# A decoder step on one Trainium2 core: fifteen input tiles made in the mixers' idle buffers, with in-place FFN input, weight sums on GpSimd and another order of the down-projection

## The chip, the cores and the metric

The kernel runs on one core of a Trainium2 chip. The core has a matrix engine (TensorE, PE in the profile; its weight loads are PEld), three elementwise engines (VectorE = DVE, ScalarE = ACT, GpSimd = POOL) and SyncE (SP), which here does nothing but issue transfers (DMA). The engines run side by side and meet through semaphores. On-chip memory is SBUF for operands and eight PSUM banks for matrix products. The metric is the device time of one execution, in microseconds.

## What is computed

One layer of a hybrid decoder, for 2048 prompt tokens and 8 x 8 sample tokens, model width 1024, all in float32:

```python
h = rmsnorm(x, norm_mix_w) * (1 + sc1) + sh1
proj = h @ w_in
qkv, z, b_raw, a_raw, sq, sk, sv = split(proj)
o_dn  = deltanet_mixer(qkv, z, b_raw, a_raw, ...)
o_swa = window_attention(sq, sk, sv, ...)
x = x + g1 * (concat(o_dn, o_swa) @ w_out)
h = rmsnorm(x, norm_ffn_w) * (1 + sc2) + sh2
u = causal_dwconv(h @ ffn_w_up) + ffn_conv_b
gate, up = split(u)
x = x + g2 * ((silu(gate) * up) @ ffn_w_down)
y = rmsnorm(x, final_norm_w)
```

`sh`, `sc` and `g` come from a small product of the conditioning vector (adaLN). The layer also returns the mixers' and the convolutions' states.

## The kernel before

**Products.** Every float32 operand is split into a rounded part and a rest ("hi" and "lo", `th`/`tl`, `wh`/`wl`), and every product is three matrix products. The split costs a copy on ACT and a subtraction on DVE or POOL for each tile. Tokens lie in the free dimension, features in the 128 partitions, so x is eight tiles (k = 0 to 7) by tokens.

**Order.** The tokens are worked in two halves (`HALVES`): the first has blocks of 512 and 512 tokens, the second of 384, 384 and 320, the last block holding the 64 sample tokens. The stages are: an opening stage (adaLN, statistics, first columns of the input projection), the rest of the first half's input projection (columns 12 to 21) beside the first steps of its mixers, the second half's input projection beside the first half's mixers, output projection and FFN up-projection of the first half, the same for the second half, then the down-projection for all tokens. `beside(steps, filler, share)` weaves elementwise-heavy mixer steps with products. Each step is a Python generator; `lockstep` advances several in turn, `chain` one after the other, `spaced` slows one down. The order in which a program line is reached is an input to a tile scheduler, which fixes each engine's instruction order before the run. Each engine, and SP's issue of transfers, then goes through its own list in order. A buffer (a tile with a tag in a pool, `bufs` of them in turn) is given out again when its last user is done; memory of a closed pool likewise.

**Places that the change touches.**

- `affine_h` (line 239) makes the projection's input h from x for one block: for each k it loads a tile of x into a "cv" buffer (line 263; there are five, `CV = 5`, in pool `gw`), scales it on DVE (line 264), adds the bias on ACT (line 266) and makes hi and lo. For odd k the subtraction is on POOL, after a separate ACT copy; for even k, ACT adds the bias while it makes hi, and DVE finishes lo. The sample tokens come as one tile `hst` (line 249), also a "cv" buffer, on which DVE does a multiplication (line 251), the bias addition and the subtraction. For the FFN, `src` can be a list of tiles that already lie in SBUF; the result still goes to a "cv" buffer.
- `second` (called when columns 12 to 21 of the first half are nearly done) calls `affine_h` for the second half: block 0 and a part of block 1 first, the rest when the first half's h is free.
- `in_evac` (from line 600) and `conv_block` (lines 530 to 548) empty a PSUM bank of the input projection and of the FFN: a copy (line 537), a scaled copy into a "cv" buffer (line 542 for the FFN) and, on DVE, the taps of the convolution (line 547). Lines 603 and 608 are the evacuation of the columns of z, sk and sv. Line 806 is a small DVE result in the mixers that a product of line 785 needs.
- The mixers' pool `mp` is opened before the first half's first mixer steps. Its tiles xz, qs, kh, kl, u, o, nl, pt and PT belong to attention and to the state scan, which start only after those steps (line 933 loads qs, 939 kl, 657 kq).
- `weight_sums` (line 1621) makes the sums of the down weights that the Winograd form of the down-projection needs: for each of 11 units two loads of 128 x 1024 into one buffer `suv`, four DVE additions of 128 x 512 (lines 1632 to 1635), two stores to `ws_d` (line 1638). Six units run in the opening stage (pool `sa`), five beside the sample tokens' mixers. On POOL in the opening stage run the square sums of `x_rstd` for the second half.
- `up_quarters` runs the second half's FFN up-projection and stores its results, token sums and E (line 1496) to HBM.
- `down_phase` (line 1648) goes through the tokens in two passes (`ip` 0 and 1), each with the seven products of the table `DOWN`. A row names the weight operand, the token operand, the token group of its form (the second is 64 tokens narrower in the second pass), whether it opens new banks, and the output blocks to which its result is added. Each product has 11 units i; a unit loads, splits and multiplies a weight tile (`wr`) and a token tile (`tr`). `T2 = B22 - T1` and `T4 = T1 + E` are formed on the way from two loads each (`tr` and `tx`, lines 1707 and 1712). Pool `ds` holds `wr`, `tr` and the splits, pool `dr` holds `tx`, the output blocks `x` (two buffers each) and the statistics. `out` adds a product to x (`residual`, line 1263 within it), and from the fourth row on a block is complete and its squares are summed. `norm` is the final norm and the store of y; it runs beside later products. Products 3 and 4 of the second pass use four banks, the others eight.

Of the kernel before, what the change touches and what calls it, by code (L numbers as in the profile page):

```python
# [22 lines left out]
P = 128  # L23
D = 1024
KT = 8
# [69 lines left out]
def kernel(  # L95
# [133 lines left out]
    def h_tile(hf, bi):  # L229
# [3 lines left out]
        return [t[:, a:a + KT * n].rearrange("p (k n) -> p k n", k=KT) for t in h_at]  # L233

    def affine_h(hb, bi, hf, branch, rB, src, ks=range(KT), pool_too=lambda k: k % 2, smp=None):

# [20 lines left out]
        for k in ks:  # L257
            h, l = hi[:, k, :np_], lo[:, k, :np_]
            t = x = gw.tile([P, 512], F32, tag="cv", name="ht", bufs=CV)[:, :np_]
            if isinstance(src, list):  # L260
                x = src[k][:, :np_]
            else:
                nc.sync.dma_start(x, src[k, :, c0:c0 + np_])
            nc.vector.scalar_tensor_tensor(t, x, S[:, k, 0:1], rB[:, :np_], ALU.mult, ALU.mult)
            if pool_too(k):
                nc.scalar.activation(t, t, AF.Identity, bias=B[:, k, 0:1], scale=1.0)
                nc.scalar.copy(h, t)
                nc.gpsimd.tensor_tensor(l, t, h.bitcast(F32), ALU.subtract)
            else:
                nc.scalar.activation(h, t, AF.Identity, bias=B[:, k, 0:1], scale=1.0)  # L270
                nc.vector.scalar_tensor_tensor(l, t, B[:, k, 0:1], h.bitcast(F32), ALU.add, ALU.subtract)  # L271
            yield True
# [1347 lines left out]

    def weight_sums(units, pool):

        tt = nc.vector.tensor_tensor
        cut = lambda t: (t[:, :D // 2], t[:, D // 2:])
        for i in units:
# [16 lines left out]

    DOWN = [("A11", "B11", 1, True, [(0, 1)]), ("S2", "T2", 1, False, [(0, 2)]), ("S3", "T3", 2, False, [(1, 1), (1, 2)]),
            ("S1", "T1", 2, True, [(1, 2)]), ("S4", "B22", 2, False, [(0, 2)]), ("A22", "T4", 1, True, [(1, 1)]),
            ("A12", "B21", 1, True, [(0, 1)])]
    NM = KT // 2

    def down_phase(ds, dr, pd):
# [28 lines left out]
        def load(tag, src, n, most, bufs):  # L1677

            raw = (dr if tag == "tx" else ds).tile([P, most], F32, tag=tag, name=tag, bufs=bufs)[:, :n]
            fetched[:] = [nc.sync.dma_start(raw, src).ins]  # L1680
            return raw
# [7 lines left out]

        w, t = {}, {}  # L1690

# [6 lines left out]
        def get_t(q, i, r):  # L1698

            if (q, i, r.start) in t:  # L1700
                return
            name = DOWN[q % ND][1]
            get = lambda tag, name, r, bufs: load(tag, t_src(q, name, i, r), r.stop - r.start, big, bufs)
            if name == "T2":
                raw, more = get("tr", "T1", r, RAWS), get("tx", "B22", slice(r.start, min(r.stop, PW)), RAWS)
                c = more.shape[1]
                nc.vector.tensor_tensor(raw[:, :c], more, raw[:, :c], ALU.subtract)
                if c < raw.shape[1]:
                    nc.scalar.mul(raw[:, c:], raw[:, c:], -1.0)
            elif name == "T4":  # L1710
                raw, more = get("tr", "T1", r, RAWS), get("tx", "E", r, RAWS)
                nc.vector.tensor_tensor(raw, raw, more, ALU.add)
            else:
                raw = get("tr", name, r, RAWS)
            t[q, i, r.start] = halves(ds, "t", raw, big, DR)

        def blocks_of(q, g=None):

            if q < ND or q % ND in (3, 4):
                return [slice(0, PW)]  # L1720
# [51 lines left out]
        for q in range(Q):  # L1772
# [26 lines left out]
            def out(m, s):  # L1799
                for og, tg in outs:  # L1800
# [3 lines left out]
                    residual(v, acc[m, s], n, n - LS if q >= ND and r.stop > PW else n, G[:, NM * og + m], v, dr)  # L1804
                    if j < 3:
                        continue
# [13 lines left out]
            def load_x():  # L1820
# [3 lines left out]
                o = need.pop(0)  # L1824
                x[o] = dr.tile([P, NM, big], F32, tag=f"x{o[0]}{o[1]}", name=f"x{o[0]}{o[1]}", bufs=2)
                with tc.issue_after(fetched[0]):
# [32 lines left out]
            elif j == 5:  # L1859
                finish = norm(*late, free[-2:], wait=2 - ip)  # L1860
            elif j == 6:
                late = (1, 0, PW, x, sums[1], cols[1])
            elif j == 2 and ip:
                finish = norm(*late, free[-2:], wait=2)
        rest(finish)
# [21 lines left out]
    with ExitStack() as main:  # L1887
# [12 lines left out]
        with ExitStack() as es:  # L1900
# [71 lines left out]
            for bi in range(2):  # L1972
                for m in range(2):
# [5 lines left out]
            chain(*[spaced(ada_cols([(c, k + q) for q in range(4)], ac, st, at_bank), 2) for c in range(2, 6) for k in (0, 4)],  # L1979
                  spaced(weight_sums(range(6), sa), 2)),  # L1980
            chain(bias_tables(sa), gates(0, h, ic["wb"], ip), *[x_rstd(1, bi, rBs[bi], sa, st_bank) for bi in range(3)]))
# [42 lines left out]
        with ExitStack() as es:  # L2024
            mp = new_pool(es, "mp", bufs=2, side="right")
            filler = inproj(0, h, ic, range(12, 22), freed=second, turn=(0, 2))
            inverse_tiles(mp)
            beside(ahead(0, mp), filler, SHARE[0])
            rest(filler)
# [21 lines left out]
        with ExitStack() as es:  # L2051
            sp = new_pool(es, "sp", side="right")
            beside(lockstep(sample_delta(sp), sample_attend(sp), weight_sums(range(6, KH), sp)), filler, SHARE[2])
        with ExitStack() as es:
# [121 lines left out]
```

## Time and profile before

| | us |
|---|---|
| runs shown, in order | 2650.94, 2656.68, 2646.79 |
| median of these | 2650.94 |
| the profiled execution | 2652.56 |
| its span in the trace | 2650.8 |
| mean granted PE clock in it | 0.99 |

The trace is of one execution on the one core, so its span, and not the median, goes with every duration read from it. In a timeline row the first number is the start in us from the begin of the span, the second the duration, and a bracket at the end gives the idle time of the engine before it and what ended that. In a row of groups (line, engine, operation, result <- operands, shape, count) the numbers after the first bar are busy us and mean ns of one, after the second bar the idle time ahead of them. SPq rows are issues of transfers by SP, DMA rows the transfers themselves. The granted clock is the share of full speed that TensorE's throttle allowed in a stretch.

### The profile page before, as it was taken

What the parts mean: (1) busy time and instruction counts of PE and PEld (TensorE: products, weight loads), DVE (VectorE), ACT (ScalarE), POOL (GpSimd) and SP (SyncE); (2) the same over time, 40 slices, a digit from 0 to 9 for tenths busy, and PEclk for the clock granted to TensorE, in tenths of its full rate; (3) what the DMA queues carried; (4) which work ended last, traced back from release to release, by engine and by line L of the source; (5) the groups of instructions that cost most, each with busy time, mean ns of one, the idle gap of its engine ahead of it and who ended that gap; (6) DMA issues with size and microseconds to landing.
All of it is one profiled execution on the core that took longest, in us unless ns stands there. A gap on an engine that the chain in (4) does not pass through costs nothing.

```text
span 2650.8 us, 45631 instructions
## 1 busy us (share of the span) xinstructions
PE 2564.9 (97%) x16424; PEld 2223.7 (84%) x16424; DVE 1838.0 (69%) x3657; ACT 1284.4 (48%) x3124; POOL 757.6 (29%) x677
## 2 busy tenths in 40 slices
PE   7999989999999899999999999999999999999998
PEld 5677878888897787777777789999999997889988
DVE  7475469887443677888868664886777666676676
ACT  5453355564342455455444353554555554554343
POOL 2031133233332412223211123335555520020012
PEclk9999989999999999999999999999999999999999
DMA  7787454334456253343226357424555459678673
GB/s 288 247 301 236 134 151 118 101 97 115 106 176 205 103 144 98 105 108 102 76 92 215 130 181 225 144 67 156 171 170 186 166 183 302 214 237 279 214 250 130
DMA packets 325327, 445.31 MB, mean 168 GB/s; under 512 B 83267, under 2 KB 207268, under 8 KB 324836
## 3 DMA queue, kind: packets, MB, share of 16 engines
q1 hardware_dynamic: 325100, 442.39, 52.7%
q8 instruction: 129, 2.11, 0.3%
q14 instruction: 98, 0.80, 0.1%
HBM read 322.74 MB, written 120.57 MB: 167 GB/s over the span
## 4 chain that ended last, share of the span: by engine, by line
PE 70%; DVE 12%; DMA 9%; ACT 3%; issue 3%; SPq 2%; POOL 1%; DVEq 0%; POOLq 0%; ACTq 0%
PE up_ps L339 15%; PE dn_ps L1795 15%; PE in_ps L339 12%; PE uq_b L1585 5%; PE op_ps L339 4%; PE uq_c L1585 2%; PE uq_u L1585 2%; PE uq_g L1585 2%; DVE ev L547 2%; PE pv_ps L1007 1%; PE uq_a L1585 1%; DMA mt<-mixd 1%; PE as_ps L970 1%; DVE w_lo L331 1%; DMA suv<-in_w_downT_dram 1%
## 5 line engine op out<-in xcount | busy, mean ns | idle before, releaser
L339 PE MATMUL in_ps<-hi,w_hi 128*128 128x512 f32 (+2 forms) x880 | 320.4, 367 | 10.0 <-ACT ev L608 5.6
L339 PE MATMUL up_ps<-hi,w_hi 128*128 128x512 f32 (+2 forms) x808 | 315.0, 390 | 7.3 <-ACT cv L542 7.3
L339 PE MATMUL in_ps<-lo,w_hi 128*128 128x512 f32 (+2 forms) x880 | 316.6, 360 | 2.4 <-DVE lo L271 2.0
L339 PE MATMUL in_ps<-hi,w_lo 128*128 128x512 f32 (+2 forms) x880 | 314.9, 358 | 0.0
L339 PE MATMUL up_ps<-lo,w_hi 128*128 128x512 f32 (+2 forms) x808 | 313.9, 388 | 0.0
L339 PE MATMUL up_ps<-hi,w_lo 128*128 128x512 f32 (+2 forms) x808 | 311.8, 387 | 0.0
L1795 PE MATMUL dn_ps<-th,wh 128*128 128x512 f32 (+2 forms) x796 | 272.2, 343 | 4.5 <-DVE x L1263 4.2
L1795 PE MATMUL dn_ps<-tl,wh 128*128 128x512 f32 (+2 forms) x796 | 272.2, 342 | 3.6 <-DVE tl L1687 3.6
L1795 PE MATMUL dn_ps<-th,wl 128*128 128x512 f32 (+2 forms) x796 | 270.8, 342 | 0.0
L331 DVE TENSOR_TENSOR w_lo<-w_raw,w_hi 128x1024 fp32r<-128x1024 f32 x115 | 145.7, 1267 | 82.8 <-ACT w_hi L330 81.3
L330 ACT CAST w_hi<-w_raw 128x1024 fp32r<-128x1024 f32 x126 | 132.0, 1047 | 145.9 <-PE op_ps L339 52.2
L339 PEld LDWEIGHTS in_ps<-hi,w_hi 128*128 128x128 f32 x880 | 166.6, 190 | 36.7 <-issue 7.8
L339 PEld LDWEIGHTS in_ps<-lo,w_hi 128*128 128x128 f32 x880 | 167.1, 190 | 26.2 <-issue 7.6
L339 PEld LDWEIGHTS up_ps<-hi,w_hi 128*128 128x128 f32 x808 | 152.6, 189 | 41.9 <-issue 8.6
L339 PEld LDWEIGHTS up_ps<-lo,w_hi 128*128 128x128 f32 x808 | 152.7, 189 | 35.1 <-issue 10.7
L339 PEld LDWEIGHTS in_ps<-hi,w_lo 128*128 128x128 f32 x880 | 166.8, 190 | 15.6 <-issue 1.6
L339 PEld LDWEIGHTS up_ps<-hi,w_lo 128*128 128x128 f32 x808 | 152.4, 189 | 31.4 <-issue 5.3
L1795 PEld LDWEIGHTS dn_ps<-th,wh 128*128 128x128 f32 x796 | 150.7, 190 | 21.9 <-DVE x L1263 3.9
L1795 PEld LDWEIGHTS dn_ps<-tl,wh 128*128 128x128 f32 x796 | 150.9, 190 | 19.1 <-DVE tl L1687 3.9
L1795 PEld LDWEIGHTS dn_ps<-th,wl 128*128 128x128 f32 x796 | 150.8, 189 | 15.6
L1686 ACT CAST wh<-wr 128x512 fp32r<-128x512 f32 x149 | 92.1, 618 | 143.7 <-PE dn_ps L1795 115.5
L547 DVE SCALAR_TENSOR_TENSOR ev<-rb,cw,ev 128x512 f32<-128x512 f32 (+2 forms) x180 | 132.3, 739 | 31.4 <-ACT ev L540 29.6
(547 smaller groups left out, 6493.5 us busy)
## 6 DMA issues: line engine op xcount, KB each, us to landing
w_raw<-in_w_upT_dram SPq DMA_DIRECT2D x50, 512.0 KB
wada<-in_w_ada_dram SPq DMA_DIRECT2D x48, 512.0 KB
w_raw<-in_w_inT_dram SPq DMA_DIRECT2D x44, 512.0 KB
wr<-ws_d SPq DMA_DIRECT2D x88, 256.0 KB
w_raw<-in_w_outT_dram SPq DMA_DIRECT2D x34, 512.0 KB
d<-act_d SPq DMA_DIRECT2D x33, 512.0 KB
wr<-in_w_downT_dram SPq DMA_DIRECT2D x66, 256.0 KB
tr<-T_d SPq DMA_DIRECT2D x66, 256.0 KB
```

Of the source, the lines that this page charges most:

```text
L330: nc.scalar.copy(hi, raw)
L331: (eng or nc.vector).tensor_tensor(lo, raw, hi.bitcast(F32), ALU.subtract)
L339: nc.tensor.matmul(ps[:, :n], a[:, k, :], b[:, k, :n], start=first is not False and k == ks[0] and i == 0, stop=last is not False and k == ...
L547: nc.vector.scalar_tensor_tensor(out, src(j), w[:, j:j + 1], out, ALU.mult, ALU.add)
L970: nc.tensor.matmul(banks[v][:, 256 * g:256 * g + 256 - P * k0], qs[:, 2 * (g0 + g) + v], t[:, v, :2 - k0].rearrange("p w j -> p (w j)"), s ...
L1007: nc.tensor.matmul(pv_ps[64 * v:64 * v + 64, :], (vprev[0], vt)[half][:, 64 * v:64 * v + 64], PT[v, half], start=half == k0, stop=half == 1)
L1585: nc.tensor.matmul(bk[t][:, :nb], u[:, k], v[:, k], start=new and k == 0 and y == 0, stop=k == KG - 1 and y == 2, skip_group_check=True)
L1686: nc.scalar.copy(h, raw)
L1795: nc.tensor.matmul(acc[m, s][:, :n], w[q, i][a][:, c], th[b][:, v], start=new and i == 0 and y == 0, stop=i == KH - 1 and y == 2, skip_gro ...
```

## The change

Four edits in one diff. (A) A generator `early_h` takes fifteen buffers of the mixers' pool under the tags of tiles that are used later, and in them loads, scales and biases the eight tiles of block 0 and the first seven of block 1 of the second half; it runs in lockstep with the mixers' first steps, and `affine_h` only makes hi and lo from a tile that is `made`. (B) Where `src` is a list, `affine_h` scales and biases the tile in place instead of writing a "cv" buffer. (C) The first six units of `weight_sums` run on GpSimd; the other five stay on VectorE. (D) The rows of `DOWN` stand in another order, with S1·T1 and S4·B22 first; their token tiles are kept in SBUF (`held`; four T1 tiles in `ds`, seven T1 and eleven B22 in `dr`), so that T2 is formed from two kept tiles and T4 from E and a kept one. `tr` moves to `dr`, `tx` goes, `x` has one buffer for each block, the four-bank products of the second pass are now 0 and 1, and the norms run one or two products later or in one chain.

```diff
+    made = {}
+
+    def early_h(pool):
...
+        def spare(tag, bufs=1, size=1):
+            t = pool.tile([P, 4 * size, P], F32, tag=tag, name="he", bufs=bufs).rearrange("p h i -> p (h i)")
+            return [t[:, 512 * i:512 * i + 512] for i in range(size)]
+
+        room = iter(spare("xz") + spare("qs", 1, 2) + spare("kh") + spare("kl") + spare("u") + spare("o")
+                    + spare("nl", 3) + spare("nl", 3) + spare("nl", 3) + spare("pt") + [spare("PT", 4)[0] for _ in range(4)])
+        for i, t in enumerate(room):
+            bi, k = divmod(i, KT)
+            c0, n = HALVES[1][bi]
+            t = made[bi, k] = t[:, :n]
+            nc.sync.dma_start(t, I["xT"][k, :, c0:c0 + n])
+            nc.vector.scalar_tensor_tensor(t, t, MOD[:, 1, k, 0:1], rB_tile(1, bi), ALU.mult, ALU.mult)
+            nc.scalar.activation(t, t, AF.Identity, bias=MOD[:, 0, k, 0:1], scale=1.0)
+            yield True
...
         for k in ks:
             h, l = hi[:, k, :np_], lo[:, k, :np_]
-            t = x = gw.tile([P, 512], F32, tag="cv", name="ht", bufs=CV)[:, :np_]
+            if (bi, k) in made:
+                t = made.pop((bi, k))
+                nc.scalar.copy(h, t)
+                (nc.gpsimd if pool_too(k) else nc.vector).tensor_tensor(l, t, h.bitcast(F32), ALU.subtract)
+                yield True
+                continue
             if isinstance(src, list):
-                x = src[k][:, :np_]
+                t = x = src[k][:, :np_]
             else:
+                t = x = gw.tile([P, 512], F32, tag="cv", name="ht", bufs=CV)[:, :np_]
                 nc.sync.dma_start(x, src[k, :, c0:c0 + np_])
             nc.vector.scalar_tensor_tensor(t, x, S[:, k, 0:1], rB[:, :np_], ALU.mult, ALU.mult)
...
-    def weight_sums(units, pool):
-
-        tt = nc.vector.tensor_tensor
+    def weight_sums(units, pool, eng):
+
+        tt = eng.tensor_tensor
...
-    DOWN = [("A11", "B11", 1, True, [(0, 1)]), ("S2", "T2", 1, False, [(0, 2)]), ("S3", "T3", 2, False, [(1, 1), (1, 2)]),
-            ("S1", "T1", 2, True, [(1, 2)]), ("S4", "B22", 2, False, [(0, 2)]), ("A22", "T4", 1, True, [(1, 1)]),
-            ("A12", "B21", 1, True, [(0, 1)])]
+    DOWN = [("S1", "T1", 2, True, [(1, 2)]), ("S4", "B22", 2, False, [(0, 2)]),
+            ("A11", "B11", 1, True, [(0, 1)]), ("S2", "T2", 1, False, [(0, 2)]), ("S3", "T3", 2, False, [(1, 1), (1, 2)]),
+            ("A22", "T4", 1, True, [(1, 1)]), ("A12", "B21", 1, True, [(0, 1)])]
+    FINAL = {(0, 2): 3, (1, 2): 4, (1, 1): 5, (0, 1): 6}
...
-            raw = (dr if tag == "tx" else ds).tile([P, most], F32, tag=tag, name=tag, bufs=bufs)[:, :n]
+            raw = (ds if tag in IN_DS else dr).tile([P, most], F32, tag=tag, name=tag, bufs=bufs)[:, :n]
...
-        w, t = {}, {}
+        w, t, held = {}, {}, {}
+        IN_DS = ["wr"] + [f"cT1_{i}" for i in range(RAWS)]
...
-            get = lambda tag, name, r, bufs: load(tag, t_src(q, name, i, r), r.stop - r.start, big, bufs)
-            if name == "T2":
-                raw, more = get("tr", "T1", r, RAWS), get("tx", "B22", slice(r.start, min(r.stop, PW)), RAWS)
-                c = more.shape[1]
-                nc.vector.tensor_tensor(raw[:, :c], more, raw[:, :c], ALU.subtract)
-                if c < raw.shape[1]:
-                    nc.scalar.mul(raw[:, c:], raw[:, c:], -1.0)
-            elif name == "T4":
-                raw, more = get("tr", "T1", r, RAWS), get("tx", "E", r, RAWS)
-                nc.vector.tensor_tensor(raw, raw, more, ALU.add)
+            n = r.stop - r.start
+            if name in ("T1", "B22"):
+                m = wide(q, 1) if name == "T1" else PW
+                held[name, i] = load(f"c{name}_{i}", t_src(q, name, i, slice(0, m)), m, big if name == "T1" else PW, 1)
+                raw = held[name, i][:, r]
+            elif name == "T2":
+                raw = dr.tile([P, big], F32, tag="tr", name="tr", bufs=RAWS)[:, :n]
+                nc.vector.tensor_tensor(raw[:, :PW], held["B22", i], held["T1", i][:, :PW], ALU.subtract)
+                if n > PW:
+                    nc.scalar.mul(raw[:, PW:], held["T1", i][:, PW:], -1.0)
             else:
-                raw = get("tr", name, r, RAWS)
+                raw = load("tr", t_src(q, "E" if name == "T4" else name, i, r), n, big, RAWS)
+                if name == "T4":
+                    nc.vector.tensor_tensor(raw, raw, held["T1", i][:, r], ALU.add)
...
-            if q < ND or q % ND in (3, 4):
+            if q < ND or q % ND in (0, 1):
...
-                    if j < 3:
+                    if j < FINAL[og, tg]:
...
-                x[o] = dr.tile([P, NM, big], F32, tag=f"x{o[0]}{o[1]}", name=f"x{o[0]}{o[1]}", bufs=2)
+                x[o] = dr.tile([P, NM, big], F32, tag=f"x{o[0]}{o[1]}", name=f"x{o[0]}{o[1]}", bufs=1)
...
             elif j == 5:
-                finish = norm(*late, free[-2:], wait=2 - ip)
-            elif j == 6:
-                late = (1, 0, PW, x, sums[1], cols[1])
-            elif j == 2 and ip:
-                finish = norm(*late, free[-2:], wait=2)
+                rest(finish or ())
+                finish = norm(*late, free[-2:])
+            elif j == 6 and not ip:
+                finish = chain(finish, norm(1, 0, PW, x, sums[1], cols[1], free[-2:], wait=2))
...
-                  spaced(weight_sums(range(6), sa), 2)),
+                  spaced(weight_sums(range(6), sa, nc.gpsimd), 2)),
...
-            beside(ahead(0, mp), filler, SHARE[0])
+            beside(lockstep(ahead(0, mp), early_h(mp)), filler, SHARE[0])
...
-            beside(lockstep(sample_delta(sp), sample_attend(sp), weight_sums(range(6, KH), sp)), filler, SHARE[2])
+            beside(lockstep(sample_delta(sp), sample_attend(sp), weight_sums(range(6, KH), sp, nc.vector)), filler, SHARE[2])
```

## The prediction

> **What bounds the kernel now.** I read the page first: busy times, then the chain that ended last.
>
> ```profile
> span 2650.8 us, 45631 instructions
> ...
> PE 2564.9 (97%) x16424; PEld 2223.7 (84%) x16424; DVE 1838.0 (69%) x3657; ACT 1284.4 (48%) x3124; POOL 757.6 (29%) x677
> ...
> PE 70%; DVE 12%; DMA 9%; ACT 3%; issue 3%; SPq 2%; POOL 1%; DVEq 0%; POOLq 0%; ACTq 0%
> ```
>
> TensorE (PE) is busy for 97% of the span, and this change takes no matrix product away. It can only win the time in which PE stands still or runs at a lowered clock. So I asked for windows of 50 us. The columns are the stretch, its length, then busy us of PE, PEld, DVE, ACT and POOL with instruction counts, granted PE clock, DMA share and GB/s. Then I asked what PE waited for: total us, times, longest.
>
> ```profile
> 200.00:250.00 50.00, 46.78 (x200) 38.27 (x200) 28.73 (x46) 19.80 (x49) 6.15 (x10) 0.93 0.70 238
> 350.00:400.00 50.00, 38.36 (x324) 33.91 (x323) 43.55 (x96) 33.88 (x106) 24.70 (x20) 0.83 0.47 127
> 900.00:950.00 50.00, 42.66 (x191) 34.90 (x191) 30.27 (x43) 23.22 (x53) 10.97 (x12) 0.93 0.36 97
> 2200.00:2250.00 50.00, 44.49 (x186) 35.64 (x185) 34.99 (x55) 20.11 (x35) 0.00 (x0) 0.97 0.92 305
> 2250.00:2300.00 50.00, 50.00 (x222) 41.42 (x221) 30.36 (x47) 21.57 (x39) 0.00 (x0) 1.00 0.71 228
> 2550.00:2600.00 50.00, 47.44 (x321) 45.15 (x320) 36.33 (x61) 25.06 (x49) 9.93 (x9) 1.00 0.62 196
> ```
>
> ```profile
> PE up_ps L339 <- ACT cv L542: 7.3, 1, 7.3
> PE z_ps L785 <- DVE T L806: 7.2, 2, 6.4
> PE in_ps L339 <- ACT ev L608: 5.6, 2, 3.6
> PE dn_ps L1795 <- DVE tl L1687: 4.6, 2, 3.6
> PE dn_ps L1795 <- DVE x L1263: 4.2, 4, 1.7
> PE in_ps L339 <- DVE ev L603: 3.2, 1, 3.2
> ```
>
> The loss of a window is its idle PE time plus 50 us times the missing clock. Hand-over of the input projection at 350: 11.6 + 8.5 = 20.1. FFN start of the first half at 900: 7.3 + 3.5 = 10.8. Near 235: 3.2 + 3.5 = 6.7. Start of the down-projection at 2200: 5.5 + 1.5 = 7.0. At 2560: 2.6. Together 47 us, about the most that this change can win; each part is aimed at one of these places. Everything below is measured against the profiled execution (2652.56 us; span 2650.8).
>
> **A, tiles made ahead (early_h).**
>
> ```profile
> 326.07 0.65 SPq L933 DMA_DIRECT2D qs<-proj  x1
> ...
> 340.88 0.59 SPq L263 DMA_DIRECT2D ht<-in_xT_dram  x1
> ...
> 347.64 0.59 SPq L939 DMA_DIRECT2D kl<-low_d  x1
> ```
>
> ```profile
> 356.29 0.57 ACT L608 COPY ev<-in_ps 128x512 f32<-128x512 f32 x1
> ```
>
> ```profile
> 376.03 1.67 DVE L251 TENSOR_TENSOR hst<-hst,MOD 128x512 f32<-128x512 f32 x1 [2.90 <-DMA hst<-in_xT_dram]
> ```
>
> ```profile
> L264 DVE SCALAR_TENSOR_TENSOR ht<-ht,MOD,sg 128x384 f32<-128x384 f32 x16 | 11.6, 745 | 11.7 <-DMA ht<-in_xT_dram 11.7
> ```
>
> ```profile
> L266 ACT ACTIVATE ht<-ht,MOD 128x384 f32<-128x384 f32 x16 | 9.8, 613 | 6.7 <-DVE ht L264 6.7
> ```
>
> Today the second half's 24 prompt tiles are loaded only from 340.9 on, through the five "cv" buffers that PSUM evacuation uses too. Two stalls follow. The evacuation at L608 comes at 356.3, long after its product, so PE waits 3.6 us for a bank. Then DVE stands 2.9 us behind the sample tile's load (hst), which got its buffer late, and PE waits 6.4 us for a small result queued behind it (L806). The change moves 15 scale operations (15 x 0.745 = 11.2 us of DVE) and the bias pass (15 x 0.613 = 9.2 us of ACT) ahead, with 15 loads of 192 KB on SP. At the hand-over each made tile keeps one ACT copy and one subtraction; on even tiles copy and subtraction replace as much work, so ACT saves only the bias pass of the odd ones. The first ten tiles need no "cv" buffer, so the evacuation should run at once, and hst gets a buffer early. The moved work lands here:
>
> ```profile
> 285.00:345.00 60.00, 60.00 (x390) 48.06 (x389) 21.23 (x59) 17.39 (x29) 1.46 (x3) 1.00 0.54 161
> ```
>
> DVE is busy 21 of 60 us there and PE never waits, so 11 us more are hidden. The cover goes only if DVE stands behind each load (a rival below). A wait is added: the mixers' first loads of qs, kh and kl (today issued 326 to 348) must now wait until the made tiles in these buffers are used up, about 343 by my estimate (two us behind ht's first load of today); xz alike. Behind them on SP queue the remaining ht loads, proj stores and weight loads, and PE needs these keys in its order before the next products. Bounds: all 20.1 won; or nothing, if PE waits for the keys as long as it now waits for the bank and hst. I take 13: both long stalls and their clock go, about 7 remain from dense DVE work.
>
> **B, FFN input in place.**
>
> ```profile
> 911.49 0.57 ACT L537 COPY rb<-up_ps 128x512 f32<-128x512 f32 x1
> ...
> 917.59 0.76 ACT L542 ACTIVATE cv<-up_ps,fcb,fcw 128x512 f32<-128x512 f32 x1
> ```
>
> L537 and L542 both read the bank that PE wants; L542 also needs a "cv" buffer, and all five hold ht. In place, none is taken, and L542 can follow L537 at about 912.1 instead of 917.6. The 5.5 us come off the stall of 7.3; some clock stays lost, since about 2 us of idling remain. Bounds 0 (L542 kept late by the ACT order) to 10.8; I take 5.5. The price of the in-place write is a wait for the tile's store to x2T, which SP issues before the norm that the affine step needs anyway: 0. The same edit in the opening stage and in the second half's FFN finds no stall on "cv": 0.
>
> **C, six weight sums on GpSimd.**
>
> ```profile
> 228.97 0.69 DVE L1632 TENSOR_TENSOR suv<-suv 128x512 f32<-128x512 f32 x1 [1.90 <-DMA suv<-in_w_downT_dram]
> ```
>
> ```profile
> 235.12 0.63 ACT L600 ACTIVATE ev<-ev 128x512 f32<-128x512 f32 x1 [5.29 <-DVE ev L547]
> ```
>
> ```profile
> L1632 DVE TENSOR_TENSOR suv<-suv 128x512 f32<-128x512 f32 x11 | 8.4, 762 | 15.0 <-DMA suv<-in_w_downT_dram 15.0
> ```
>
> ```profile
> L1438 POOL TENSOR_TENSOR S<-rawg 128x512 f32<-128x512 f32 x17 | 22.2, 1305 | 43.7 <-DMA rawg<-in_w_upT_dram 43.7
> ```
>
> ```profile
> 232.88 0.32 SPq L1638 DMA_DIRECT2D ws_d<-suv  x1
> ...
> 238.35 0.93 SPq L657 DMA_DIRECT2D kq<-proj  x2
> ```
>
> The last unit's four sums, with a wait of 1.9 us for their load, stand on DVE ahead of three convolution taps; ACT waits 5.3 us for those and PE 3.2 for L603. Without them (1.9 + 4 x 0.69 = 4.7 us) that stall is nearly closed. DVE loses 24 sums, 18 us; GpSimd gains 24 x 1.305 = 31 us. One unit's four sums take 5.2 us instead of about 3.0, and load, sums and store follow each other in one buffer, so over the last two or three units the last store goes out 5 to 6 us later, near 238.4. That is just when SP today issues kq, on which the first mixer work of PE waits. The slack is used up, not overdrawn. Behind a waiting sum on GpSimd stand the square sums of the second half's norm. Bounds -3 to +6.7; I take 4.
>
> [...] The rows say a ratio of 1305 to 762 ns, 1.7, and an engine 29% busy.
>
> **D, order and kept tiles of the down-projection.** The loads fall from 44 to 0 (T2) and from 44 to 22 (T4), but the phase is not bound by bytes except at its start.
>
> ```profile
> 2176.94 0.40 PE L1795 MATMUL dn_ps<-th,wh 128*128 128x512 f32 x1
> ```
>
> ```profile
> 2172.85 0.93 SPq L1680 DMA_DIRECT2D tr<-act_d  x1
> ...
> 2189.30 0.32 SPq L1496 DMA_DIRECT2D E_d<-d  x1
> 2189.71 0.41 SPq L1827 DMA_DIRECT2D x<-x2T  x1
> ```
>
> ```profile
> 2197.02 4.86 DMA wr<-ws_d
> ...
> 2213.69 2.83 DMA tr<-T_d
> ```
>
> ```profile
> L1687 DVE TENSOR_TENSOR tl<-tr,th 128x512 fp32r<-128x512 f32 x110 | 76.5, 695 | 1.3 <-ACT th L1686 1.3
> ```
>
> Today ten of eleven token tiles of the first product are in by 2173, since "tr" rotates in memory that is free early (pool ds). T2's double loads then start only at 2190, and PE waits at 2200 and 2212. In the new order only four T1 tiles lie in ds; the other seven are in dr, and today dr's first load (x) goes out at 2189.7, behind the last E store. PE, at 50/222 = 0.225 us a product and 12 products a unit (2.7 us), uses up four units by 2187.8. The fifth tile, issued at 2189.7, lands after 2.8 to 4.9 us (the rows above) and needs a cast, whose wait was 1.3 us over all of L1687 and which I estimate at 0.6, and a subtraction of 0.695: 2193.8 to 2195.9. So the old stall goes, and a new one of 6 to 8 us comes earlier, with 1.5 for the clock. I book -2 (8 to 9 instead of 7.0). Bounds: -8 if the 1 MB x load also holds up the sixth tile, +7 if SP issues the dr loads when PE leaves the up-projection at 2176.9.
>
> At 2560 the evacuation stands behind T4's additions, one of which waits for its load:
>
> ```profile
> 2558.62 0.76 DVE L1712 TENSOR_TENSOR tr<-tr,tx 128x576 f32<-128x576 f32 x1 [1.11 <-DMA tr<-T_d]
> ```
>
> One of its two loads goes, so +1 of 2.6. But the change from four to eight banks moves to the second product and S3T3, with two results for each bank, now stands before it: -3 to +2.6. The single buffer of x waits for y stores a whole product earlier: 0.
>
> **Sum.** 13 + 5.5 + 4 - 2 + 1 = 21.5; 2652.56 - 21.5 = 2631. The median of the three runs (2650.94) is 1.6 below the profiled execution, so I forecast 2630.
>
> [...]
>
> **The rivals.**
> - The hand-over stall only moves (A = 0): PE reaches the mixers' score products and waits for keys that SP could not load. For it: kl went out at 347.6, and now the whole set has to go after 343. Against: the made tiles in those buffers are the first to be used. 2630 + 13 = 2643.
> - The dr loads go out early (D = +7): 2630 - 9 = 2621. Against it is the SP order above.
> - Slower: the early tiles' scale operations stand in DVE's queue behind their own loads, and evacuation and mixer work behind them. Price of one: between 0.73 us (11.7 over 16 at L264) and the 2.9 of hst, so 11 to 44 for 15; I take 27, and 11 of work. It decides from the point at which 60% of these 38 us, 23, reaches PE, with A's gain gone: 2630 + 13 + 23 = 2666. Against it: DVE is idle for 39 of the 60 us.
> - The change does not do what it says, because the order of issue leaves the early tiles for the hand-over and B's L542 late: about 2649.
>
> **How the numbers follow.** Forecast 0.58 (2620 to 2641), keys late 0.18, dr early 0.14, no effect 0.05, DVE standing 0.05. A difference of 0.5%, about 13 us, is what a measurement of this kernel can tell from no change. Faster by more (below 2637.7): seven eighths of the forecast and dr early, 0.65. Within: the rest of the forecast, keys late, no effect: 0.30. Slower: 0.05. The range from 2615 to 2645 leaves out the last two, the outer part of dr early and part of keys late.
>
> **What would show it.** A: PE idle and clock between 350 and 390, no wait on L608, hst landed before DVE asks. B: L542 right behind L537, PE's wait there below 3 us. C: no DVE wait on suv before 240, kq issued no later than 239. D: PE idle near 2188, not near 2200. Wrong would be: new waits of PE between 240 and 345, or score products that wait for kh or kl.

## The result, and the profile after

| kernel | median us (runs) | the kernel before beside it | ratio, 95% interval |
|---|---|---|---|
| changed | 2626.11 (6) | 2648.74 (6) | 0.991 [0.9894, 0.9927] |
| changed, measured again | 2627.28 (4) | 2649.08 (17) | 0.9917 [0.99, 0.9934] |

The change makes the kernel 0.9% faster. It took 22.6 us off, by the medians; 20.9 were forecast (2650.94 to 2630). The profiled execution of the changed kernel took 2624.72 us with a span of 2622.9; before it was 2652.56 and 2650.8.

The windows of the changed kernel at the five places (the FFN's start has moved to 885, the down-projection's to 2153):

```profile
200.00:250.00 50.00, 48.65 (x222) 39.92 (x221) 26.46 (x31) 16.51 (x36) 25.43 (x23) 1.00 0.68 235
350.00:400.00 50.00, 47.17 (x410) 42.75 (x409) 44.62 (x110) 31.36 (x104) 22.00 (x19) 1.00 0.46 136
850.00:900.00 50.00, 46.60 (x202) 37.46 (x201) 32.58 (x41) 23.70 (x40) 21.03 (x13) 0.97 0.33 108
2150.00:2200.00 50.00, 44.92 (x193) 36.78 (x192) 31.03 (x44) 20.88 (x38) 0.20 (x1) 0.93 0.78 279
2550.00:2600.00 50.00, 48.94 (x363) 48.68 (x361) 38.56 (x79) 25.57 (x56) 12.68 (x11) 1.00 0.49 161
```

Idle time and missing clock together, as in the prediction: 1.4 us (6.7 before), 2.8 (20.1), 4.9 (10.8), 8.6 (7.0), 1.1 (2.6). That is 18.8 where 47.2 were, 28.4 less, and the span is 27.9 shorter. So read in this pair of traces, each part has won about what it was booked with: C 5.3 (4 booked), A 17.3 (13), B 5.9 (5.5), D -1.6 and 1.5 (-2 and 1). For C this is an effect of the window's edges: small waits of the changed kernel lie just outside 200 to 250, and from 160 to 260 the loss is 6.2 us before and 5.9 after. And a second trace of the changed kernel has a span of 2627.7, 4.8 longer, so one pair of traces settles no term of this size.

What TensorE waited for in the changed kernel (total us, times, longest):

```profile
PE dn_ps L1825 <- ACT th L1713: 5.1, 1, 5.1
PE in_ps L365 <- DVE ev L629: 2.1, 1, 2.1
PE up_ps L365 <- DVE lo L297: 1.9, 1, 1.9
PE up_ps L365 <- ACT sg L568: 1.5, 1, 1.5
PE kq_ps L697 <- DMA kq<-proj: 1.2, 1, 1.2
PE z_ps L811 <- DVE T L832: 1.1, 1, 1.1
```

The long waits for L542, L806, L608 and L603 are gone. The new one of 5.1 us is the one that the prediction set near 2188. The key loads, which one rival feared, are issued sooner than before (the last two kl from 345.1 on; the last one at 347.6 before), and the sample tile is issued at 351.7 instead of 369.5:

```profile
345.08 1.23 SPq L965 DMA_DIRECT2D kl<-low_d  x2
...
351.66 0.45 SPq L268 DMA_DIRECT2D hst<-in_xT_dram  x1
```

In the timeline of ScalarE at the FFN's start, the scaled evacuation follows the copy at once, as B meant:

```profile
890.67 0.57 ACT L563 COPY rb<-up_ps 128x512 f32<-128x512 f32 x1
891.14 0.78 ACT L568 ACTIVATE sg<-up_ps,fcb,fcw 128x512 f32<-128x512 f32 x1
```

One pair of traces can't say whether these parts are independent terms. The experiments ask that.

### The profile page after: what moved, and what is told of

Its sections match the earlier page's. It is cut to its first block, busy times and chain, and to the rows that moved or that the text cites. A ratio compares the mean times of both kernels' runs of the same rounds, so it can differ in the third digit from the quotient of the medians.

```text
span 2622.9 us, 45390 instructions
## 1 busy us (share of the span) xinstructions
PE 2553.1 (97%) x16424; PEld 2216.3 (84%) x16424; DVE 1840.1 (70%) x3633; ACT 1288.9 (49%) x3140; POOL 795.7 (30%) x708
## 4 chain that ended last, share of the span: by engine, by line
PE 74%; DVE 10%; DMA 7%; ACT 3%; issue 2%; POOL 2%; SPq 1%; POOLq 0%; DVEq 0%; ACTq 0%
PE up_ps L365 17%; PE dn_ps L1825 16%; PE in_ps L365 12%; PE op_ps L365 5%; PE uq_b L1611 5%; PE uq_c L1611 2%; PE uq_u L1611 2%; PE uq_g L1611 2%; PE pv_ps L1033 1%; DVE ev L573 1%; PE uq_a L1611 1%; DMA mt<-mixd 1%; PE as_ps L996 1%; PE u_ps L811 1%; DVE w_lo L357 1%
## 5 line engine op out<-in xcount | busy, mean ns | idle before, releaser
L365 PEld LDWEIGHTS up_ps<-lo,w_hi 128*128 128x128 f32 x808 | 152.3, 188 | 37.4 <-issue 10.7
L573 DVE SCALAR_TENSOR_TENSOR ev<-rb,cw,ev 128x512 f32<-128x512 f32 (+2 forms) x180 | 140.3, 785 | 38.6 <-ACT ev L566 36.9
```

The source lines that it names most:

```text
L365: nc.tensor.matmul(ps[:, :n], a[:, k, :], b[:, k, :n], start=first is not False and k == ks[0] and i == 0, stop=last is not False and k == ...
L573: nc.vector.scalar_tensor_tensor(out, src(j), w[:, j:j + 1], out, ALU.mult, ALU.add)
```

## The experiments

**Each part taken out of the changed kernel.** For `no_early` only the woven-in generator goes; `no_inplace` and `sums_dve` take back one hunk; `old_down` has the old table and `down_phase`.

```diff
-            beside(lockstep(ahead(0, mp), early_h(mp)), filler, SHARE[0])
+            beside(ahead(0, mp), filler, SHARE[0])
```

> The changed kernel with part A alone undone (no tile of the second half is made ahead). Theory: A is worth what the matching products show in the two traces between 350 and 540 us, about 14 us, and nothing of it is given back later: 2626 + 14 = 2640 us, with TensorE idle for 9 to 12 us and a granted clock near 0.83 in the window around the hand-over, the wait on L634 (the evacuation) and the one behind the sample tile's load back. Rival: a good part of the hand-over's loss is absorbed by the mixers' weaving later, so the time is 2630 to 2634.

```diff
+            t = x = gw.tile([P, 512], F32, tag="cv", name="ht", bufs=CV)[:, :np_]
             if isinstance(src, list):
-                t = x = src[k][:, :np_]
+                x = src[k][:, :np_]
```

> The changed kernel with part B alone undone (FFN input goes through the cv buffers again). Theory: the single wait of TensorE for the scaled evacuation at the start of the first half's FFN comes back with its clock loss, 7 to 8 us: 2633 to 2634 us. By the prediction's own term it would be 5.5: 2631.6. Rival: A has already freed that place (other timing), B is worth nothing: 2626.

```diff
-                  spaced(weight_sums(range(6), sa, nc.gpsimd), 2)),
+                  spaced(weight_sums(range(6), sa, nc.vector), 2)),
```

> The changed kernel with part C alone undone (all weight sums on VectorE). Theory: the wait of 3.2 us for the taps near 233 comes back and the small waits of the changed kernel near 246 and 255 (1.2 for kq, 2.1 for a bank) go: net 3 to 4 us, 2629 to 2630 us. Rival: what C won near 233 is spent again by 260 because GpSimd's last unit is late: 2626 us.

> The changed kernel with part D alone undone (old order of the down-projection, no kept tiles). Theory: the wait at the start moves from the fifth unit of the first product (5.1 us, clock 0.93) back to the second product (3.6 and 1.4 us): no net change there; the waits of 0.9 and 1.7 us in the last third come back with about 3 us: 2629 us. Rival: D's late gain is a chance of one trace, 2626 us; or D costs at the start, 2624.

The changed kernel was then run again on the chip, as a base:

> The changed kernel once more, as the base for the runs beside it. Every theory: 2624 to 2629 us, with one wait of about 5 us at the fifth unit of the down-projection's first product and a granted clock near 0.93 behind it; if that wait comes and goes between executions of the same kernel, it is a matter of transfers and not of the order.

| taken out | median us (runs) | ratio to before, 95% interval | more than 2627.28 |
|---|---|---|---|
| A (no_early) | 2651.32 (12) | 1.0003 [0.999, 1.0016] | 24.0 |
| B (no_inplace) | 2631.58 (6) | 0.9936 [0.9915, 0.9958] | 4.3 |
| C (sums_dve) | 2634.74 (7) | 0.9943 [0.9923, 0.9963] | 7.5 |
| D (old_down) | 2637.02 (8) | 0.9953 [0.9935, 0.997] | 9.7 |

These add up to 45.5, twice what the whole change wins. A, C and D cost more to lose than was expected, B less: without A nothing is left of the gain, though B, C and D are still in. The kernel before took 2650.04 beside these four and 2649.08 beside the base, and the intervals of B and C overlap that of the changed kernel, so these two differences are the uncertain ones. The parts are no independent terms, and the next runs put A, C and D alone into the kernel before (B alone was not run).

**A, C and D alone, and A's loads without its arithmetic.** `loads_only` keeps the fifteen early loads of the changed kernel but leaves scale and bias to `affine_h`, which was meant to bring them to the hand-over.

> The kernel before with part A alone (fifteen tiles made ahead). Theory: A takes the loss of 20.1 us at the hand-over (11.6 idle, 8.5 clock) down to about 3, as in the changed kernel: 2650 - 17 = 2633 us. The prediction's term was 13: 2637. Rival, from the run without A that came out no faster than the kernel before: A is worth 25 us and the other parts nothing without it: 2625 us.

```diff
             t = made[bi, k] = t[:, :n]
             nc.sync.dma_start(t, I["xT"][k, :, c0:c0 + n])
-            nc.vector.scalar_tensor_tensor(t, t, MOD[:, 1, k, 0:1], rB_tile(1, bi), ALU.mult, ALU.mult)
-            nc.scalar.activation(t, t, AF.Identity, bias=MOD[:, 0, k, 0:1], scale=1.0)
...
             if (bi, k) in made:
-                t = made.pop((bi, k))
...
+                t = x = made.pop((bi, k))
+            elif isinstance(src, list):
```

> The changed kernel in which the fifteen early tiles are only loaded ahead; their scale on VectorE and bias on ScalarE come at the hand-over again. It tells apart what A wins by: buffers that are free and data that is there, or elementwise work that is moved. Theory (buffers and loads): most of A's gain stays, 2629 to 2633 us, with the bank evacuation at L634 on time and the sample tile early. Rival (moved work: 11 us of VectorE and 6 to 9 of ScalarE at a place where both are dense): most of A's gain goes, 2640 to 2648 us, with TensorE waiting for VectorE results between 345 and 400.

> The kernel before with part C alone (six weight sums on GpSimd). The changed kernel without A came out as slow as the kernel before, though B, C and D were in it, and its hand-over lost more than before's (28.7 against 20.5 us, idle and clock together, from 340 to 420). Theory: C wins 3 to 4 us in the opening stage, but without A it makes the hand-over 7 us worse: 2650 + 4 = 2654 us. Rival (the parts add up): 2650 - 4 to -8 = 2642 to 2646 us.

> The kernel before with part D alone. Theory (as the two traces show it): nothing at the start of the phase, 3 us in the last third: 2647 us. Rival, from the run with the old down-projection, whose median was 10 above the changed kernel's: D is worth 10 us by itself, 2640 us. Either way the trace should show the wait of about 5 us at the fifth unit of the first product, and none in the second.

| kernel | median us (runs) | before beside it | ratio, 95% interval |
|---|---|---|---|
| A alone (only_early) | 2641.30 (10) | 2649.08 (17) | 0.9972 [0.9959, 0.9986] |
| changed, scale and bias late (loads_only) | 2637.74 (8) | 2649.08 (17) | 0.9946 [0.993, 0.9962] |
| C alone (only_sums) | 2660.54 (5) | 2650.36 (15) | 1.0041 [1.0029, 1.0054] |
| D alone (only_down) | 2645.19 (11) | 2650.36 (15) | 0.9979 [0.997, 0.9989] |

A alone wins 7.8 us and not the 17 expected. C alone loses 10.2; where A is in, C wins 7.5. `loads_only` lies 10.5 above the changed kernel, but it did not take apart what it was made for: the scheduler put the scale operations early all the same. These are the fifteen of the changed kernel and of `loads_only` (shortest, median and longest in ns, then the first and the last start):

```profile
L251 DVE SCALAR_TENSOR_TENSOR he<-he,MOD,sg x15: 584/615/967, 249.9 to 261.7; 128x384 f32<-128x384 f32 x15
L284 DVE SCALAR_TENSOR_TENSOR he<-he,MOD,sg x15: 581/616/1219, 250.8 to 264.6; 128x384 f32<-128x384 f32 x15
```

Seven of the fifteen bias passes stayed early too (252 to 264); the other eight became part of the making of hi. So nearly the same instructions, at nearly the same places, take 10.5 us longer, and from 340 to 420 `loads_only` loses 2.9 us, as little as the changed kernel. What differs is the order of issue (on TensorE from some 258 us on). What the moved arithmetic is worth by itself stays untested.

To see where, I split the traces at the first product of the second half's input projection (the hand-over) and the first of the output projection. The rows of the latter, in the order before, A alone, C alone, changed:

```profile
799.42 0.80 PE L339 MATMUL op_ps<-mixh,w_hi 128*128 128x512 f32 x1 [2.41 <-ACT ev L608]
```

```profile
792.04 0.50 PE L365 MATMUL op_ps<-mixh,w_hi 128*128 128x512 f32 x1 [1.90 <-ACT ev L634]
```

```profile
806.97 0.40 PE L339 MATMUL op_ps<-mixh,w_hi 128*128 128x512 f32 x1
```

```profile
779.53 0.50 PE L365 MATMUL op_ps<-mixh,w_hi 128*128 128x512 f32 x1 [0.27 <-ACT ev L634]
```

| in the trace, us | to the hand-over | from there to the output projection |
|---|---|---|
| neither A nor C (before; only_down) | 356.9; 355.5 | 442.5; 442.8 |
| A (only_early; sums_dve) | 356.3; 357.9 | 435.8; 435.0 |
| C (only_sums; no_early) | 359.1; 356.7 | 447.9; 445.8 |
| A and C (changed; again; old_down; no_inplace) | 351.8; 354.3; 354.9; 351.7 | 427.7; 428.4; 426.4; 427.9 |
| A and C (ds8; t1_twice; t1_late, see below) | 352.4; 356.2; 352.7 | 430.2; 429.5; 431.4 |
| A and C (loads_only) | 355.7 | 437.2 |

This table is the main finding, and but for `loads_only` it repeats itself in kernels that differ elsewhere. After the hand-over, A alone takes 7 us off, C alone adds 3 to 5, both together take 11 to 16 off; `loads_only` has both and stands with the kernels that have A alone. Windows of 40 us behind the hand-over show the place (columns as in the prediction), for the kernel before:

```profile
340.00:380.00 40.00, 30.02 (x250) 27.14 (x249) 28.05 (x64) 28.25 (x86) 16.24 (x12) 0.86 0.65 178
380.00:420.00 40.00, 38.05 (x243) 33.62 (x242) 39.26 (x102) 22.20 (x69) 17.51 (x15) 0.92 0.33 99
```

with C alone:

```profile
340.00:380.00 40.00, 30.89 (x245) 27.34 (x243) 25.01 (x58) 25.75 (x78) 13.42 (x10) 0.91 0.64 181
380.00:420.00 40.00, 33.04 (x210) 28.65 (x211) 39.10 (x94) 21.67 (x68) 19.96 (x16) 0.83 0.26 76
```

and with A alone:

```profile
340.00:380.00 40.00, 39.57 (x301) 35.77 (x301) 31.40 (x71) 31.11 (x96) 19.98 (x16) 1.00 0.54 154
380.00:420.00 40.00, 38.49 (x282) 33.86 (x281) 38.13 (x109) 22.74 (x78) 13.49 (x14) 1.00 0.39 119
```

VectorE is busy for 38 to 39 of the 40 us after 380 in all three, but that alone doesn't set TensorE's loss: in that window TensorE loses 13.8 us with C alone (7.0 idle, 6.8 clock), 5.2 before and 1.5 with A alone. With C alone its waits from 340 to 425, but for the one at L608, are on results of the mixers' chains that come out of VectorE's full list:

```profile
PE v_ps L701 <- DVE Kt L686: 5.8, 1, 5.8
PE in_ps L339 <- ACT ev L608: 3.3, 1, 3.3
PE u_ps L785 <- DVE Y L833: 3.0, 1, 3.0
PE kq_ps L671 <- DVE AM L712: 1.8, 2, 1.0
```

All kernels with A lose 1.9 to 3.4 us from 340 to 420; without A they lose 20.7 (before), 20.3 (D alone), 26.5 (C alone) and 28.5 (no_early). So A's gain lies here: alone it wins 18.8 us in these two windows, of which the whole stretch keeps 7. A part of the rest is that 43 more of TensorE's products stand behind the hand-over (3379 against 3336).

What C adds to A does not lie in these windows: they lose 1.9 and 2.0 us with A and without C, 2.8 to 3.4 with both. A part lies ahead of the hand-over (the first column), a part behind 420: from there to the output projection TensorE is idle for 13.6 and 12.1 us with A alone and 14.5 in `loads_only`, and for 6.5 to 11.5 in the other kernels with both. What C changes there is no instruction: the order of issue is another from the opening stage on, on TensorE from some 140 us. Why the scheduler's new order is worse at the hand-over without A and better elsewhere with it was not found out; that stays open.

C's own work in the opening stage shows the price that the prediction named, in the list of GpSimd's groups of the changed kernel:

```profile
L1660 POOL TENSOR_TENSOR suv<-suv 128x512 f32<-128x512 f32 x6 | 9.9, 1644 | 0.4
L1659 POOL TENSOR_TENSOR suv<-suv 128x512 f32<-128x512 f32 x6 | 8.7, 1452 | 0.3
L1658 POOL TENSOR_TENSOR suv<-suv 128x512 f32<-128x512 f32 x6 | 8.5, 1416 | 21.6 <-DMA suv<-in_w_downT_dram 21.6
L1661 POOL TENSOR_TENSOR suv<-suv 128x512 f32<-128x512 f32 x6 | 8.5, 1409 | 0.4
```

The 24 sums take 35.6 us, 1.48 each and not 1.305. Against the 0.762 of VectorE's row in the kernel before that is a ratio of 1.9, where my rows gave 1.7. And in place of the wait of 3.2 us for L603, C alone has one of 2.6 for kq and 2.4 at rb_ps, in the second half's norm, whose square sums share GpSimd with the weight sums (that they were late by these was argued, not measured):

```profile
PE kq_ps L671 <- DMA kq<-proj: 2.6, 1, 2.6
PE rb_ps L222 <- DVE dg L218: 2.4, 3, 1.4
```

**The start of the down-projection.** Its length, from its first product to the end of the span, separates D from the rest. The first products' rows for the changed kernel, D alone, and the changed kernel without D:

```profile
2152.67 0.40 PE L1825 MATMUL dn_ps<-th,wh 128*128 128x512 f32 x1
```

```profile
2175.64 0.40 PE L1799 MATMUL dn_ps<-th,wh 128*128 128x512 f32 x1
```

```profile
2156.05 0.40 PE L1821 MATMUL dn_ps<-th,wh 128*128 128x512 f32 x1
```

With spans of 2622.9, 2645.0 and 2632.0 that is 470.3, 469.4 and 476.0 us; before it was 473.8. Over all traces the old order takes 473.7 to 476.0 and the new 469.4 to 470.8 (but for the three kernels that follow). So D wins about 4 us, whatever stands ahead of it; the medians put it at 5.2 alone and 9.7 in the whole, and the traces don't show where the rest would be. The start costs 1.6 us more than before; the gain is late: the two waits for L1263 near 2563 (0.9 and 1.7 us) don't come back.

If the stall of 5.1 us is due to the T1 tiles in `dr`, whose loads go out only behind the last E store, more of them in `ds` should cure it:

```diff
-        IN_DS = ["wr"] + [f"cT1_{i}" for i in range(RAWS)]
+        IN_DS = ["wr"] + [f"cT1_{i}" for i in range(8)]
```

> The changed kernel with eight instead of four T1 tiles in pool ds, so that their loads need not wait until pool dr's memory is free. Theory (prediction's D): the wait of 5.1 us at the fifth unit and its clock loss of about 3 go, since eight units last 21.6 us and the first load into dr is issued 12 us after the product's start: 2626 - 8 = 2618 us, the first product without a wait. Rival: the transfers themselves are late (DMA share 0.8 in that stretch), and the wait appears at the ninth unit or at the start of the second product: 2624 to 2627 us.

It took 2636.73 us (4 runs; ratio 0.9954 [0.9938, 0.9969]), 9 worse. SP's queue shows why; first of the changed kernel:

```profile
2132.55 0.32 SPq L1707 DMA_DIRECT2D wr<-ws_d  x1
...
2164.27 0.32 SPq L1522 DMA_DIRECT2D E_d<-d  x1
2164.68 0.41 SPq L1707 DMA_DIRECT2D cT<-T_d  x1
```

then of `ds8`:

```profile
2163.90 0.32 SPq L1522 DMA_DIRECT2D E_d<-d  x1
2164.27 0.45 SPq L1707 DMA_DIRECT2D wr<-ws_d  x1
```

All loads of the larger `ds`, the weights too, stand behind the last E store; as I read it, the pool now reaches into memory that the up-projection still uses. TensorE waited 13.4 us for the first product, so this layout can't say whether the cause was right. The next kernel leaves `ds` as large as it was: the first product reads T1 through `tr` buffers in `ds`, and the kept tiles are loaded a second time.

```diff
-        IN_DS = ["wr"] + [f"cT1_{i}" for i in range(RAWS)]
+        IN_DS = ["wr", "tr"]
...
-            if name in ("T1", "B22"):
+            if name == "T1" and q == 0:
+                raw = load("tr", t_src(q, name, i, r), n, big, RAWS)
+            elif name in ("T1", "B22"):
...
+                if q == 1:
+                    held["T1", i] = load(f"cT1_{i}", t_src(0, "T1", i, slice(0, PW)), PW, big, 1)
...
-                raw = dr.tile([P, big], F32, tag="tr", name="tr", bufs=RAWS)[:, :n]
+                raw = ds.tile([P, big], F32, tag="tr", name="tr", bufs=RAWS)[:, :n]
```

> The changed kernel with another home for the first product's tiles: in the first pass the first product reads its T1 tiles through the four tr buffers, which lie in pool ds again as in the kernel before, and the kept T1 tiles are loaded a second time, all into dr, during the second product (11 loads more). With eight kept tiles in ds every load of that pool stood behind the last E store; here ds keeps its size. Theory: the loads of ten T1 tiles go out before the phase, the wait of 5 us at the fifth unit and its clock loss go, 2627 - 8 = 2619 us. Rival: the wait moves to the second product, whose B22 tiles share the transfers with the second T1 loads: 2624 to 2628 us.

It took 2627.13 us (4 runs; 0.9907 [0.9891, 0.9922]), the same as the changed kernel. The wait at the fifth unit is gone, so its cause was right: T1 loads that went out only behind the last E store. But a wait of 1.9 us comes at the end of the first product and one of 4.4 in the second, for a residual (L1289). Parts of the chain that ended that wait, from the critical path of this trace:

```profile
2185.03 7.93 DMA wr<-ws_d
...
2192.98 0.63 ACT wh L1713
...
2194.93 0.67 DVE x L1289
```

The residual stands on VectorE behind the split of a weight tile whose load of 256 KB took 7.9 us. That its x was late, as the next expectation has it, this trace does not show. As the DMA share stood above 1 there (1.04 from 2180 to 2190, 1.05 from 2190 to 2200), the last kernel moved the second loads one product later, to `q == 2`:

> As the kernel that loads T1 twice, but with the second loads one product later (during A11 B11, where the DMA share was 0.4 in the changed kernel) and not during the second product, where the share stood at 1.04 and TensorE waited 4.5 us for a residual whose x load was late. Theory (the wait moved into crowded transfers): both waits of the down-projection's start (5.1 us in the changed kernel; 1.9 and 4.5 in the kernel with the early second loads) go or shrink below 2 us in all, and the time is 2627 - 7 = 2620 us. Rival (the x loads of 1 MB behind the last E store are late in any case): 2625 to 2628 us with a wait of 3 to 5 us near the end of the first or in the second product.

2628.22 us (6 runs; 0.993 [0.9915, 0.9945]): no gain, as the rival had it, with one wait of 1.2 us and one of 4.5, which ended at 2199.3. But the edit moved the second loads less far than was meant; they still went out ahead of that end, from here on:

```profile
2189.79 0.32 SPq L1707 DMA_DIRECT2D cT<-T_d  x1
2190.52 0.32 SPq L1707 DMA_DIRECT2D wr<-ws_d  x1
```

Here too the residual stood behind the split of a weight tile, and not behind x:

```profile
2196.50 0.62 ACT L1713 CAST wh<-wr 128x512 fp32r<-128x512 f32 x1 [3.52 <-DMA wr<-ws_d]
```

The windows:

```profile
2180.00:2190.00 10.00, 8.54 (x37) 6.50 (x36) 1.99 (x3) 1.76 (x3) 0.00 (x0) 1.00 1.05 391
2190.00:2200.00 10.00, 5.52 (x25) 4.27 (x24) 3.25 (x5) 2.39 (x5) 0.00 (x0) 1.00 1.05 386
2200.00:2210.00 10.00, 9.90 (x37) 7.55 (x36) 6.54 (x10) 3.94 (x7) 0.00 (x0) 0.83 1.04 384
```

The transfers stand at 384 to 391 GB/s with a share above 1, in the first of these windows before any second T1 load was issued. As I read it, what waits behind the last E store (x of 1 MB each, B22, weights) is more than can land before it is used; a kernel in which the second loads come clear of this stretch was not run. These two kernels' down-projections took 471.4 and 470.6 us, no less than the changed kernel's. I found no version that beats the changed kernel.

## Why the prediction came out right, point by point

- **The total.** Forecast 2630 (2615 to 2645), measured 2626.1 and 2627.3. The sign and the size were right, and so were the places of A's, B's and D's waits. That the size is right is in part luck (see the sum). The range also holds the kernels without B, C or D (2631.6, 2634.7, 2637.0), not the one without A.
- **A, booked 13, bounds 0 to 20.1.** The window 350 to 400 wins 17.3 in the changed kernel; about 7 were to remain and 2.8 did. Both long stalls went, also in A alone, so the mechanism (buffers and the sample tile early) was right; buffers and early data were not told apart. Yet alone A wins only 7.8: the prediction did not ask what comes after its window, where a good part is given back. The rival of late keys was wrong: the last kl was issued by 346.3, and TensorE waited for none of these loads. The rival of a standing VectorE came true in small. The early tiles were not scaled from 285 to 345, as booked, but from 250 to 262, and there VectorE stood for their loads, with an evacuation (L629) and a product of TensorE behind them:

```profile
249.85 3.05 DVE L251 SCALAR_TENSOR_TENSOR he<-he,MOD,sg 128x384 f32<-128x384 f32 x5 [6.71 <-DMA he<-in_xT_dram]
...
256.79 0.68 DVE L629 SCALAR_TENSOR_TENSOR ev<-ev,in_ps 128x512 f32<-128x512 f32 x1
```

```profile
257.53 0.50 PE L365 MATMUL in_ps<-hi,w_hi 128*128 128x512 f32 x1 [2.14 <-DVE ev L629]
```

  That is a new wait between 240 and 345, which the prediction had named as a sign of being wrong. It cost 2.1 us (2.4 in the repeat), not the 38 of the rival; from 260 to 340 TensorE was busy for 80.00 of 80 us.
- **B, booked 5.5, bounds 0 to 10.8.** Taking it out costs 4.3 us, and the wait of 7.3 us for L542 comes back in full. Mechanism and size were right, the size within the noise of the medians.
- **C, booked 4, bounds -3 to 6.7.** This step failed as it was put. The wait for L603 went, as argued, but with C alone two others of 2.4 and 2.6 took its place; the prediction had named both (kq's store, square sums behind the sums) and called the slack used up, not overdrawn. From 160 to 260 idle time and missing clock are 8.0 us with C alone against 6.2 before: in its own stage C wins nothing. The large effects lie where the prediction did not look: the time grows by 10.2 us with C alone, for the larger part at the hand-over, and falls by 7.5 with A, ahead of the hand-over and behind 420. The first is outside the bounds; the second is too, but by less than its noise.
- **D, booked -2 and +1.** The stall at the fifth unit came as predicted, in place (10.7 us after the first product, as four units of 2.7) and size (5.1 us and 3.5 of clock, 8.6 in the window; 8 to 9 were booked). The late gain was 2.6 to 3 and not 1: the feared wait for two results on each bank did not come. In all D wins about 4.
- **The sum.** Four terms were added as if each stood alone. Alone, A, C and D are worth 7.8, -10.2 and 5.2, which with B's 4.3 would be 7 us. The remaining 15 of the 22.6 come from parts acting together, by the traces mostly A and C (A and C without B and D were not run). That the sum was right rests on both being in and on an order of issue that nobody foresaw: that is luck.

## What to carry to other kernels

Measure a part both alone and as the only one left out: where the two differ, as 7.8 and 24 for A, the parts are no independent terms. Here an edit changed the order of issue of everything behind it, and 10 us were lost twice with little or no other change at the place of the loss: with C alone, and in `loads_only`. A small term is uncertain by that much, wherever it is booked. Look also whether an experiment moved what it was to move: two here did not, or not far enough. And before moving a wait ahead of a burst of loads, count the bytes that wait behind the same event: here TensorE waited 5.1 us in the changed kernel and 6.5 and 5.9 in the two that load T1 twice, beside transfers at 380 to 391 GB/s in all three.

## What was unexpected of the hardware

- In the down-projection's start the DMA share reads above 1 (1.04 to 1.05) at 384 to 391 GB/s for 30 us in the last of these kernels, from 2180 to 2210. The page's slices of 66 us hide it: in the changed kernel, with 1.04 and 1.05 from 2170 to 2190, the slice that holds this stretch stands at 7 tenths.
- After the wait of 13.4 us in `ds8`, the granted clock was 0.75 in the ten us from 2170 on, 2.5 us of missing clock behind the wait:

```profile
2160.00:2170.00 10.00, 0.54 (x1) 0.50 (x2) 4.85 (x7) 1.48 (x3) 0.00 (x0) 0.57 0.65 218
2170.00:2180.00 10.00, 10.00 (x35) 7.97 (x34) 6.12 (x10) 6.16 (x10) 0.00 (x0) 0.75 1.05 391
```

- The clock was also below 1 around shorter waits. With C alone it was 0.94 from 230 to 260, where TensorE's 2.6 us of idle time are the wait for kq. The wait of 3.3 us for L608 ended at 359.1; the clock was 0.99 from 340 to 360, and 0.84 from 360 to 380, where TensorE was idle for another 5.8 us.
